# A finished right operand for the output product, made behind FFN 1 and kept in DRAM

## The chip, the cores and the metric

The kernel runs on one core of a Trainium2 chip. Compared is the device time of one execution in microseconds, the median of several runs of the whole layer, inputs and output in DRAM.

## The reference

One layer over 1024 tokens of width 1024, float32. The change touches the product with `w_out`; what it moves lies behind the first feed-forward block.

```python
h = h + 0.5 * swiglu(rms_norm(h, n1), w_gate1, w_up1, w_down1)           # FFN 1
z = rms_norm(h, nm) @ w_in                                              # q, k, v and two gates
merged = sigmoid(gA) * (yA @ w_branch_a) + sigmoid(gB) * (yB @ w_branch_b)
h = h + merged @ w_out                                                  # the output product
h = h + 0.5 * swiglu(rms_norm(h, n2), w_gate2, w_up2, w_down2)           # FFN 2
y = rms_norm(h, nf)
```

## The kernel before

**Precision.** Every operand of a large product is kept as two halves, hi (a cast to float32r) and lo (the rest), and a product of 128 x 128 by 128 x 512 is three matmuls into one PSUM bank: L149 hi by hi, L151 and L153 hi by lo and lo by hi. `split` makes the halves of a 128 x 512 operand: ACT casts hi (L95), DVE subtracts lo (L98). In FFN 1 the same is done by L325 and L332.

**Products.** Large products are Strassen-like: seven products P1 to P7 of quarter matrices in place of eight. Class `Down` does one for each W_down and one, the *merge*, for `w_out`. The merge's inner size is 4 blocks, so it has 28 entries (7 products by 4), taken in the order P2, P1, P5, P6, P3, P7, P4. For an entry `prep` makes a pair of tiles, the left operand `s` (a quarter of `merged`, or a sum that was put into `left_d`) and the right operand `t` (a block of `w_out`, or a difference of blocks), each 128 x 1024 with hi and lo side by side. Pairs stand in a ring of six: four of `ws` tiles, two inside the large tile `ar` (`pair_slots`). `run` prepares entry e + 5 before it multiplies entry e, and each entry is four times three matmuls. The last four entries are multiplied in `tail`, later.

**The right operand before.** `load_blocks` fetches the four quarters of `w_out` during branch A in eight transfers of 512 KB (L567) into two `ar` tiles. `prep` forms the differences in place on DVE: one subtraction per entry of P5 (L590) and P3 (L595), two per entry of P6 (L592, L593), so 16 in all; then it splits the left and the right operand (L95, L98).

**FFN 1.** It has 154 products, and after each `behind_ffn1(n)` is called with the number n that are left. It slips work in that belongs to later stages. 28 *items* (16 branch weights, 12 halves of gate weights) are each fetched (256 KB, L756 on SP), split two products later (ACT L760, DVE L761, both into small tiles `hs`, six in all), and put one product later by two transfers of 256 KB (L768, Pool's queue) to `wab_d` or `wg_d`. One item is begun every third product. From n = 10 on, `down.at_end` loads and prepares the product with W_down of FFN 1, one part of which stands in the two tiles `xs`.

**Order.** Instructions run in program order on each engine. `pin` and the calls above set that order; each engine waits for what its next instruction needs and nothing overtakes. DMAs are started by SP (loads and some stores) and Pool (puts), in order on each. The weights of FFN 1 are loaded by SP (L295), and its products are evicted by ACT (L477 and others) and DVE (L497 and others) out of PSUM banks; of the banks, the one in which P6 ends is written again soonest: P7's first matmul goes into it one product after P6's last.

Of the kernel before, what the change touches and what calls it, by code (L numbers as in the profile page):

```python
# [13 lines left out]
ALU = mybir.AluOpType  # L14
# [17 lines left out]
def f32v(ap):  # L32
    return ap.bitcast(F32)


@with_exitstack
def trunk_kernel(ctx, tc, x, xt, n1, wg1, wu1, wd1, nm, win, rpb, sink, wa, wb, wo,
                 n2, wg2, wu2, wd2, nf, c_rope, c_mask_a, c_mask_b, out):
    nc = tc.nc

# [13 lines left out]
    def nm_(s):  # L54
        uid[0] += 1
        return f"{s}_{uid[0]}"
# [32 lines left out]
    def ws4():  # L89
        return main.tile([P, 1024], F32R, tag="ws", bufs=8, name=nm_("ws"))  # L90
# [431 lines left out]
    def pair_slots(s):  # L522
        return slot(s), slot(s + 1)
# [8 lines left out]
    class Down:  # L532
# [2 lines left out]

        ORDER = ("P2", "P1", "P5", "P6", "P3", "P7", "P4")

        def __init__(self, n, w, scale, place, left=None, dram=None, loads={}, ring=(22, 24, 26), shift=0, late=False):
            self.n, self.w, self.scale, self.place, self.left, self.dram, self.loads = n, w, scale, place, left, dram, loads
            self.seq = [(k, p) for k in self.ORDER for p in range(n)]  # L540
            self.dk = [k for k in self.ORDER if k in dram]
            self.nd = (n + 1) // 2
            self.raw, self.nraw, self.done, self.ent, self.tiles, self.loaded = {}, 0, 0, {}, {}, {}
            self.TAIL, self.late = min(n, 5), late
            self.ring, self.shift, self.RING = ring, shift, 4 + len(ring)
            self.W = self.Y = None
# [32 lines left out]
        def prep(self, e):  # L579
            k, p = self.seq[e]  # L580
            if k in self.dram:
                d = self.dk.index(k) * self.nd + p // 2
                self.load_left(d + 3)
                left = self.raw[d][:, p % 2, :]
            else:
                left = self.left(k, p)
            b11, b12, b21, b22 = [self.blocks(n, p)[:, 0, :] if n in self.loaded else None for n in ("B11", "B12", "B21", "B22")]
            eng = nc.gpsimd if self.n > self.RING else nc.vector
            if k == "P5":
                nc.vector.tensor_tensor(b11, b12, b11, op=ALU.subtract)  # L590
            elif k == "P6":
                nc.vector.tensor_tensor(b11, b22, b11, op=ALU.subtract)  # L592
                eng.tensor_tensor(b12, b22, b12, op=ALU.subtract)  # L593
            elif k == "P3":
                eng.tensor_tensor(b21, b21, b11, op=ALU.subtract)  # L595
            i = (e + self.shift) % self.RING
            s, t = (ws4(), ws4()) if i < 4 else pair_slots(self.ring[i - 4])
            split(s[:, :512], s[:, 512:], left, None, self.late)
            split(t[:, :512], t[:, 512:], dict(B11=b11, B12=b12, B21=b21, B22=b22)[SOURCE[k]], None, self.late)
            self.ent[e] = s, t  # L600
# [145 lines left out]
    def hs(dt):  # L746
        return main.tile([P, 512], dt, tag="hs", bufs=6, name=nm_("hs"))
# [16 lines left out]
    def wab_put(i):  # L764
        g, half = divmod(i - 2 * NC8, 2)
        for k, a in enumerate(cast.pop(i)):
            dst = wab_d[i, :, k * 512:k * 512 + 512] if g < 0 else wg_d[g, k, :, half * 512:half * 512 + 512]
            nc.gpsimd.dma_start(dst, f32v(a))  # L768

    def behind_ffn1(n):  # L770
        down.at_end(n)
        if n <= 60 and spread:
            nc.sync.dma_start(*spread.pop(0))
        for e, f in ((3, wab_put), (2, wab_split), (0, wab_fetch)):
            i, k = divmod(100 - e - n, 3)
            if k == 0 and 0 <= i < 2 * (NC8 + len(gates)):
                f(i)

    hg = hidden(wg1, wu1, behind_ffn1, (8, 10, 9, 11), by_hand=True)

# [736 lines left out]
    def quarter(k, p):  # L1517
        m = merged(p + (4 if k in ("P2", "P4") else 0))
        return m[:, :512] if k in ("P1", "P2") else m[:, 512:]

    place = dict(B11=[(4, p) for p in range(4)], B21=[(4, 4 + p) for p in range(4)],
                 B12=[(1, p) for p in range(4)], B22=[(1, 4 + p) for p in range(4)])
    loads = {t: [lambda d, t=t: load_h(t)] for t in range(NTT)}
    loads[0].append(lambda d: d.load_left(2))
    down = Down(4, wo[0], 0.5, place, quarter, {k: left_d[i] for i, k in enumerate(("P5", "P6", "P3", "P7"))},
                loads, (8, 10), late=True)

    def combine(p):
        a11, a12, a22 = [quarter(k, p) for k in ("P1", "P2", "P4")]
# [7 lines left out]
    for i, dc in enumerate(a_order):  # L1537
        r = mix.pop(("ra", i))
        if i + 2 < NC8:
            a_fetch(i + 2)  # L1540
        if i >= 2:
            branch_a(i)
        if i % 2 == 0:
            down.load_blocks(("B21", "B11", "B12", "B22")[i // 2])
        if i + 3 == NC8:
            new_ar(2)
        if i + 1 == NC8:
            down.prep_until(2)
        bs, mm = a_mm[i]
        drain(mm)  # L1550
        if i + 6 < NC8:
            fetch_w(NC8 + i + 6)
        if i + 2 < NC8:
            a_open(i + 2)
        for n in range(2):
            sl = slice(n * 512, (n + 1) * 512)
            nc.vector.scalar_tensor_tensor(out=r[:, sl], in0=r[:, sl], scalar=1.0, in1=bs[n], op0=ALU.add, op1=ALU.mult)
        nc.vector.tensor_tensor(merged(dc), merged(dc), r, op=ALU.add)
        if i % 2:
            combine(i // 2)  # L1560
# [139 lines left out]
```

## Time and profile before

| | us |
|---|---|
| median of 3 runs | 1919.72 |
| lowest and highest run | 1918.26, 1920.03 |
| span of the profiled execution | 1915.6 |
| PE busy in it | 1905.7 (99%) |
| DVE, ACT, POOL busy | 1451.9 (76%), 947.5 (49%), 306.5 (16%) |
| DMA moved | 338.57 MB, 177 GB/s |

The profiled execution is given by its span, from its first instruction to its last; that span is 4.1 us shorter than the median of the runs, and what lies around it (launch and end) is in the runs' time and not in the profile. PE is TensorE's matmuls, whose ends are modelled, so a busy PE may still be spaced wider than it could be; the spacing of their starts tells. The waits of an engine are listed with what released them.

On the trace's clock FFN 1 runs from about 11 to 430 us, the branch products end at 1195.94, and the 24 entries of the merge before its tail run from there to about 1261.

### The profile page before, as it was taken

The page shows a single profiled execution, that of the slowest core. Times are in us where ns is not written, and L with a number is a line of the kernel's source. Part 1 is how long each engine was busy: PE and PEld are TensorE (multiplying, and loading weights), DVE is VectorE, ACT ScalarE, POOL GpSimd, SP SyncE. Part 2 cuts the span into 40 slices and gives each one's busy share as a digit, 9 for nine tenths or more (in the row PEclk, how much of TensorE's full clock was granted, in tenths as well). Part 3 has the DMA queues.
Part 4 walks back from the last instruction along what each step waited for, and adds up shares of the span by engine and source line. Part 5 has one row for each costly group of instructions (what it writes and reads, how often), then busy time and mean ns, then how long its engine had stood idle before and what let it go on. Part 6 is the DMA issues. An engine that isn't in the chain of part 4 may idle for free.

```text
span 1915.6 us, 25959 instructions
## 1 busy us (share of the span) xinstructions
PE 1905.7 (99%) x9044; PEld 1597.7 (83%) x9044; DVE 1451.9 (76%) x2545; ACT 947.5 (49%) x1847; POOL 306.5 (16%) x477
## 2 busy tenths in 40 slices
PE   9999999999999999999999999999999999999998
PEld 7888888888888888898898888888888888888886
DVE  8988766668967778755887997999675566569864
ACT  7533444444446543444888983475333333344453
POOL 0012222214400112211112201010110001005111
PEclk9999999999999999999999999999999999999999
DMA  7256656677354277753648978444432323492341
GB/s 269 95 175 217 231 200 219 205 277 284 115 180 141 105 213 236 226 176 127 176 117 228 283 225 309 171 154 133 142 110 97 118 88 110 157 357 86 119 140 61
DMA packets 174211, 338.57 MB, mean 177 GB/s; under 512 B 17280, under 2 KB 79616, under 8 KB 174080
## 3 DMA queue, kind: packets, MB, share of 16 engines
q1 hardware_dynamic: 140752, 235.18, 37.5%
q0 software_dynamic: 32464, 100.69, 15.6%
q8 instruction: 71, 1.16, 0.3%
q10 hardware_dynamic: 864, 1.05, 0.2%
q14 instruction: 60, 0.49, 0.1%
HBM read 230.43 MB, written 108.19 MB: 177 GB/s over the span
## 4 chain that ended last, share of the span: by engine, by line
PE 97%; DVE 1%; DMA 1%; ACT 0%; issue 0%; POOL 0%; SPq 0%; POOLq 0%; DVEq 0%; ACTq 0%
PE g L149 18%; PE g L153 17%; PE g L151 17%; PE d L153 12%; PE d L151 12%; PE d L149 12%; PE d L1438 2%; PE g L1457 1%; PE d L1417 1%; PE g L1452 1%; PE d L1418 1%; PE d L142 1%; DVE ar L98 0%; DMA fx<-in_xt_dram 0%; DMA fx<-v_d 0%
## 5 line engine op out<-in xcount | busy, mean ns | idle before, releaser
L149 PE MATMUL g<-ar,ws 128*128 128x512 f32 x1064 | 404.6, 393 | 0.0
L151 PE MATMUL g<-ar,ws 128*128 128x512 f32 x1064 | 401.8, 390 | 0.0
L153 PE MATMUL g<-ar,ws 128*128 128x512 f32 x1064 | 400.4, 390 | 0.0
L149 PE MATMUL d<-ar,ws 128*128 128x512 f32 x728 | 281.6, 390 | 0.4 <-ACT ar L908 0.4
L151 PE MATMUL d<-ar,ws 128*128 128x512 f32 x728 | 281.1, 389 | 0.6 <-DVE ar L910 0.6
L153 PE MATMUL d<-ar,ws 128*128 128x512 f32 x728 | 281.2, 389 | 0.0
L153 PEld LDWEIGHTS g<-ar,ws 128*128 128x128 f32 x1064 | 199.6, 188 | 41.6
L151 PEld LDWEIGHTS g<-ar,ws 128*128 128x128 f32 x1064 | 199.6, 188 | 41.0
L149 PEld LDWEIGHTS g<-ar,ws 128*128 128x128 f32 x1064 | 196.6, 188 | 35.9 <-DVE fa L1030 0.3
L332 DVE TENSOR_TENSOR ws<-raw,ws 128x512 fp32r<-128x512 f32 x216 | 147.6, 688 | 92.9 <-ACT ws L325 92.0
L325 ACT CAST ws<-raw 128x512 fp32r<-128x512 f32 x216 | 132.6, 620 | 149.6 <-PE g L153 67.0
L151 PEld LDWEIGHTS d<-ar,ws 128*128 128x128 f32 x728 | 136.7, 188 | 29.8 <-DVE ar L910 1.2
L149 PEld LDWEIGHTS d<-ar,ws 128*128 128x128 f32 x728 | 136.5, 188 | 28.9 <-ACT ar L908 0.9
L153 PEld LDWEIGHTS d<-ar,ws 128*128 128x128 f32 x728 | 136.6, 188 | 28.7 <-DVE ws L332 0.5
L95 ACT CAST ws<-raw 128x512 fp32r<-128x512 f32 x98 | 61.0, 623 | 119.2 <-PE d L153 59.9
L98 DVE TENSOR_TENSOR ws<-raw,ws 128x512 fp32r<-128x512 f32 x98 | 73.2, 747 | 44.3 <-ACT ws L95 44.2
L444 POOL DMA_DIRECT2D hid<-fx x91 | 49.2, 540 | 349.6 <-DVE fx L504 221.6
L98 DVE TENSOR_TENSOR ws<-ar,ws 128x512 fp32r<-128x512 f32 x114 | 93.5, 828 | 14.6 <-ACT ws L95 14.6
L95 ACT CAST ar<-raw 128x512 fp32r<-128x512 f32 (+1 forms) x81 | 54.0, 670 | 83.5 <-PE g L151 51.5
L149 PE MATMUL g<-ws,ws 128*128 128x512 f32 x232 | 90.9, 392 | 0.0
L153 PE MATMUL g<-ws,ws 128*128 128x512 f32 x232 | 90.4, 390 | 0.0
L151 PE MATMUL g<-ws,ws 128*128 128x512 f32 x232 | 90.3, 389 | 0.0
(344 smaller groups left out, 3830.9 us busy)
## 6 DMA issues: line engine op xcount, KB each, us to landing
raw<-hid SPq DMA_DIRECT2D x70, 512.0 KB
hid<-fx POOLq DMA_DIRECT2D x91, 256.0 KB, 2.7
ar<-in_ffn_w_down_dram SPq DMA_DIRECT2D x32, 512.0 KB
raw<-in_ffn_w_up_dram SPq DMA_DIRECT2D x31, 512.0 KB
raw<-in_ffn_w_gate_dram SPq DMA_DIRECT2D x27, 512.0 KB
hid<-fa POOLq DMA_DIRECT2D x51, 256.0 KB, 2.7
ar<-zs_d POOLq DMA_DIRECT2D x48, 256.0 KB, 7.5
raw<-in_w_in_dram SPq DMA_DIRECT2D x20, 512.0 KB
```

Source lines behind the costliest of these rows:

```text
L95: hi = nc.scalar.copy(dst_hi, src)
L98: (eng or nc.vector).tensor_tensor(dst_lo, src, f32v(dst_hi), op=ALU.subtract)
L142: nc.tensor.transpose(pt[:, c * P:(c + 1) * P], xs[:, (half * 4 + c) * P:(half * 4 + c + 1) * P], ident)
L149: nc.tensor.matmul(b, lhs[0], r[0], start=first, stop=False, **kw)
L151: nc.tensor.matmul(b, lhs[0], r[1], start=False, stop=False, **kw)
L153: nc.tensor.matmul(b, lhs[1], r[0], start=False, stop=last, **kw)
L325: nc.scalar.copy(w[0][:, :512], a)
L332: nc.vector.tensor_tensor(w[0][:, 512:], a, f32v(w[0][:, :512]), op=ALU.subtract)
L444: nc.gpsimd.dma_start(hid[PRODUCTS.index(p), i], src)
L1417: nc.tensor.matmul(b[:, :nw], un["q"][s], un["kd"][s][:, k0 * P:k1 * P], start=True, stop=False)
L1418: nc.tensor.matmul(b[:, :nw], un["q"][s], un["kl"][s][:, k0 * P:k1 * P], start=False, stop=True)
L1438: nc.tensor.transpose(pt[:, i * P:(i + 1) * P], un["pr"][s][:, i * P:(i + 1) * P], ident)
```

## The change

Three things are changed.

1. The items behind FFN 1 are begun every second product and no longer every third: item i is fetched at n = 108 - 2i (before: 100 - 3i). They end near n = 51, before: n = 16.
2. Behind them, from n of about 52 on, the right operand of the output product is made. For each of the four blocks p, four fetches of 256 KB bring the quarters of `w_out` into `hs` tiles (`wo_fetch`); then one entry is made every 1.5 products: a subtraction on DVE where the entry is a difference (16 in all, `wo_split`), a cast on ACT and a subtraction on DVE into one of three tiles that are idle there (`split_out`: two `xs` and the tile `gain`), and one product later one transfer of 512 KB, hi and lo side by side, on Pool's queue to `wo_d` (`wo_put`). The last put is called at n = 8.
3. In the merge, `prep` loads the finished `t` of an entry from `wo_d` with one transfer of 512 KB on SP and splits only the left operand. The eight loads of `w_out` in branch A are gone.

```diff
-            b11, b12, b21, b22 = [...]          # prep, before: always
+            if self.right is not None:
+                i = (e + self.shift) % self.RING
+                s, t = (ws4(), ws4()) if i < 4 else pair_slots(self.ring[i - 4])
+                nc.sync.dma_start(f32v(t), self.right[PRODUCTS.index(k), p])
+                split(s[:, :512], s[:, 512:], left, None, self.late)
+                self.ent[e] = s, t
+                return
...
+    wo_d = dram.tile([len(PRODUCTS), 4, P, 1024], F32, name="wo_d")
+    def halves_out():
+        nout[0] += 1
+        if nout[0] % 3 == 0:
+            return const.tile([P, 1152], F32R, tag="gain", bufs=1, name=nm_("made"))[:, :1024]
+        return main.tile([P, 1024], F32R, tag="xs", bufs=2, name=nm_("made"))
+    def split_out(key, src):
+        n = src.shape[1]
+        o = cast[key] = halves_out()[:, :2 * n]
+        pin(nc.scalar.copy(o[:, :n], src))
+        pin(nc.vector.tensor_tensor(o[:, n:], src, f32v(o[:, :n]), op=ALU.subtract))
+    def put_out(key, dst):
+        nc.gpsimd.dma_start(dst, f32v(cast.pop(key)))
+    def wo_fetch(p):
+        for n, (r0, c0) in dict(B21=(4, 0), B11=(0, 0), B22=(4, 512), B12=(0, 512)).items():
+            wo[n, p] = hs(F32)
+            nc.sync.dma_start(wo[n, p], wout[0][(r0 + p) * P:(r0 + p + 1) * P, c0:c0 + 512])
+    def wo_split(k, p):
+        for d, a, b in dict(P5=(("B11", "B12", "B11"),), P7=(("B12", "B22", "B12"),), P6=(("B11", "B22", "B11"),),
+                            P4=(("B21", "B21", "B11"),)).get(k, ()):
+            pin(nc.vector.tensor_tensor(wo[d, p], wo[a, p], wo[b, p], op=ALU.subtract))
+        split_out((k, p), wo[SOURCE[k], p])
...
+    for i in range(2 * (NC8 + len(gates))):
+        for e, f in ((3, wab_put), (2, wab_split), (0, wab_fetch)):
+            later(108 - 2 * i - e, f, i)
+    step = [50 - 1.5 * k for k in range(29)]
+    for p in range(4):
+        later(step[7 * p] + 2, wo_fetch, p)
+        for j, k in enumerate(("P2", "P1", "P3", "P5", "P7", "P6", "P4")):
+            later(step[7 * p + j], wo_split, k, p)
+            later(step[7 * p + j] - 1, wo_put, k, p)
...
-        for e, f in ((3, wab_put), (2, wab_split), (0, wab_fetch)):
-            i, k = divmod(100 - e - n, 3)
-            if k == 0 and 0 <= i < 2 * (NC8 + len(gates)):
-                f(i)
+        for f, *a in background.get(n, ()):
+            f(*a)
...
-    down = Down(4, wo[0], 0.5, place, quarter, {...}, loads, (8, 10), late=True)
+    down = Down(4, None, 0.5, {}, quarter, {...}, loads, (8, 10), late=True, right=wo_d)
...
-        if i % 2 == 0:
-            down.load_blocks(("B21", "B11", "B12", "B22")[i // 2])
```

How this moves the instructions is seen at three places. The order on PE is the same before and after, matmul for matmul.

ACT, in the last third of FFN 1, around copies of PSUM banks `d` and `g` into `fx` (L477); L325 is the cast of FFN 1's own weights. Before:

```order
L477 COPY fx_75<-d_2410 128x512
L325 CAST ws_2425<-fa 128x512
L477 COPY fx_76<-d_2428 128x512
L760 CAST hs_2443<-hs_2404 128x512
L325 CAST ws_2447<-raw_2177 128x512
L477 COPY fx_76<-g_2321 128x512
L325 CAST ws_2472<-raw_2468 128x512
L477 COPY fx_77<-g_2343 128x512
```

After:

```order
L477 COPY fx_75<-d_2511 128x512
L325 CAST ws_2528<-fa 128x512
L477 COPY fx_76<-d_2531 128x512
L793 CAST made_2546<-hs_2499 128x512
L325 CAST ws_2549<-raw_2260 128x512
L477 COPY fx_76<-g_2412 128x512
L325 CAST ws_2571<-raw_2567 128x512
L477 COPY fx_77<-g_2432 128x512
L793 CAST made_2588<-hs_2501 128x512
```

At this place a cast of the output product's first entry stands where an item's cast stood; the items are done by then, and from here a cast of L793 comes every 1.5 products, at times two of them in a row, where before one of L760 came every third.

SP, at the start of the merge: L576 (after: L577) loads sums from `left_d`, L1512 (L1568) loads rows of h, L295 loads weights of FFN 2. Before:

```order
L576 DMA raw_11129<-left_d 128x2x512
L1512 DMA fa<-h_d 128x1024 x2
L576 DMA raw_11131<-left_d 128x2x512
L576 DMA raw_11133<-left_d 128x2x512
L576 DMA raw_11206<-left_d 128x2x512
L1512 DMA fa<-h_d 128x1024 x2
L576 DMA raw_11256<-left_d 128x2x512
```

After:

```order
L577 DMA raw_11278<-left_d 128x2x512
L591 DMA ws_11285<-wo_d 128x1024
L591 DMA ws_11290<-wo_d 128x1024
L1568 DMA fa<-h_d 128x1024 x2
L591 DMA ws_11314<-wo_d 128x1024
L591 DMA ws_11332<-wo_d 128x1024
L577 DMA raw_11280<-left_d 128x2x512
L577 DMA raw_11282<-left_d 128x2x512
L577 DMA raw_11349<-left_d 128x2x512
L591 DMA ws_11352<-wo_d 128x1024
L591 DMA ws_11378<-wo_d 128x1024
```

The loads of finished operands (L591) stand between the loads of sums and of h, two to a load of sums, in the one queue.

DVE, in the merge, from the splits of P5's entries to the eviction of P1 out of bank `g` into `fx`. Before:

```order
L98 TENSOR_TENSOR ar_11005<-ar_10855,ar_11005 128x512
L590 TENSOR_TENSOR ar_10855<-ar_10970,ar_10855 128x512
L98 TENSOR_TENSOR ar_11005<-raw_11131,ar_11005 128x512
L592 TENSOR_TENSOR ar_10855<-ar_10970,ar_10855 128x512
L98 TENSOR_TENSOR ar_11005<-ar_10855,ar_11005 128x512
L593 TENSOR_TENSOR ar_10970<-ar_10970 128x512
L98 TENSOR_TENSOR ws_11298<-raw_11133,ws_11298 128x512
L98 TENSOR_TENSOR ws_11299<-ar_10855,ws_11299 128x512
L631 SCALAR_TENSOR_TENSOR fx_10848<-g_11231,fx_10848 128x512
```

After:

```order
L639 SCALAR_TENSOR_TENSOR fx_11012<-d_11276,fx_11012 128x512
L98 TENSOR_TENSOR ws_11351<-raw_11278,ws_11351 128x512
L98 TENSOR_TENSOR ws_11377<-raw_11278,ws_11377 128x512
L98 TENSOR_TENSOR ar_11158<-raw_11280,ar_11158 128x512 x2
L639 SCALAR_TENSOR_TENSOR fx_11009<-g_11372,fx_11009 128x512
```

The differences (L590, L592, L593) and the second split of each entry are gone from between the evictions; one split per entry stays.

## Rows read from the trace of the kernel before

**Rows 1.** The page: span, then busy time of each engine over the whole span.

```profile
span 1915.6 us, 25959 instructions
PE 1905.7 (99%) x9044; PEld 1597.7 (83%) x9044; DVE 1451.9 (76%) x2545; ACT 947.5 (49%) x1847; POOL 306.5 (16%) x477
```

**Rows 2.** All waits of PE: line, awaited, releaser: us in total, times, longest.

```profile
PE g L829 <- POOL ident masks.py:199: 1.5, 1, 1.5
PE d L151 <- DVE ar L910: 0.6, 2, 0.3
PE d L149 <- ACT ar L908: 0.4, 1, 0.4
PE d L1438 <- DVE ws L98: 0.2, 1, 0.2
```

**Rows 3.** Windows: us, then PE, PEld, DVE, ACT, POOL busy, clock, DMA share, GB/s.

```profile
133.00:293.00 160.00, 160.00 (x708) 132.48 (x707) 122.78 (x193) 63.88 (x110) 35.06 (x65) 1.00 0.62 210
293.00:408.00 115.00, 115.00 (x509) 95.24 (x508) 76.73 (x119) 47.92 (x84) 24.28 (x45) 1.00 0.63 212
...
1195.00:1260.00 65.00, 65.00 (x291) 53.67 (x290) 64.11 (x103) 30.51 (x56) 5.84 (x10) 1.00 0.52 182
...
1195.00:1217.00 22.00, 22.00 (x97) 17.94 (x96) 21.85 (x35) 9.24 (x17) 3.24 (x6) 1.00 0.73 256
```

**Rows 4.** Timeline of PE in the merge: start, duration, engine, line, operation, tiles.

```profile
1195.94 0.39 PE L149 MATMUL d<-ws,ws 128*128 128x512 f32 x1
...
1198.66 0.39 PE L149 MATMUL d<-ws,ws 128*128 128x512 f32 x1
...
1204.10 0.39 PE L149 MATMUL d<-ws,ws 128*128 128x512 f32 x1
1204.40 0.50 PE L151 MATMUL d<-ws,ws 128*128 128x512 f32 x1
...
1207.03 0.39 PE L149 MATMUL g<-ar 128*128 128x512 f32 x1
```

**Rows 5.** Timeline of DVE in the merge, same columns.

```profile
1203.67 0.68 DVE L98 TENSOR_TENSOR ws<-ar,ws 128x512 fp32r<-128x512 f32 x1
```

**Rows 6.** Groups by line, DVE and ACT, 293 to 408 us: busy, mean ns | idle before.

```profile
L761 DVE TENSOR_TENSOR hs<-hs,hs 128x512 fp32r<-128x512 f32 x12 | 8.3, 688 | 9.2 <-ACT hs L760 9.2
L760 ACT CAST hs<-hs 128x512 fp32r<-128x512 f32 x12 | 7.4, 617 | 0.0
```

**Rows 7.** Waits of ACT and of SP's queue in FFN 1, 133 to 408 us.

```profile
ACT ws L325 <- PE d L153: 46.7, 30, 2.1
...
SPq L756 <- DVE hs L761: 65.9, 13, 8.6
```

**Rows 8.** Timeline of ACT in FFN 1; in brackets the idle time before.

```profile
296.98 0.59 ACT L477 COPY fx<-g 128x512 f32<-128x512 f32 x1 [1.10 <-PE g L153]
```

**Rows 9.** DMA issues, 130 to 420 us: transfer, queue, count, KB each, us to landing.

```profile
wab_d<-hs POOLq DMA_DIRECT2D x32, 256.0 KB, 3.9
```

**Rows 10.** Groups by line, DVE and ACT, around the merge.

```profile
L98 DVE TENSOR_TENSOR ws<-ar,ws 128x512 fp32r<-128x512 f32 x25 | 16.5, 683 | 0.0
L590 DVE TENSOR_TENSOR ar<-ar,ar 128x512 f32<-128x512 f32 x4 | 2.7, 682 | 0.0
L95 ACT CAST ws<-ar 128x512 fp32r<-128x512 f32 x24 | 14.1, 618 | 22.6 <-PE d L153 9.5 <-DVE ar L592 6.7 <-DVE ar L590 5.8
```

**Rows 11.** DMA of 1150 to 1260 us in 40 slices (tenths, GB/s); a put.

```profile
DMA  9999988699899920468559945500614146055890
GB/s 326 399 411 386 366 317 311 191 339 388 353 410 419 411 94 0 164 206 268 229 159 384 421 180 197 188 2 0 197 36 154 19 171 191 4 186 180 346 408 25
DMA packets 9065, 25.95 MB, mean 236 GB/s; under 512 B 922, under 2 KB 922, under 8 KB 9056
...
left_d<-fa POOLq DMA_DIRECT2D x16, 256.0 KB, 5.6
```

**Rows 12.** Timeline of SP's queue at the merge.

```profile
1215.20 16.00 SPq L576 DMA_DIRECT2D raw<-left_d  x4
```

More of the change, by code (lines that the diff above doesn't have):

```diff
@@ L36, in trunk_kernel @@
 @with_exitstack
-def trunk_kernel(ctx, tc, x, xt, n1, wg1, wu1, wd1, nm, win, rpb, sink, wa, wb, wo,
+def trunk_kernel(ctx, tc, x, xt, n1, wg1, wu1, wd1, nm, win, rpb, sink, wa, wb, wout,
                  n2, wg2, wu2, wd2, nf, c_rope, c_mask_a, c_mask_b, out):
@@ L536, in trunk_kernel, with __init__ @@
         ORDER = ("P2", "P1", "P5", "P6", "P3", "P7", "P4")
-        def __init__(self, n, w, scale, place, left=None, dram=None, loads={}, ring=(22, 24, 26), shift=0, late=False):
+        def __init__(self, n, w, scale, place, left=None, dram=None, loads={}, ring=(22, 24, 26), shift=0, late=False, right=None):
+            self.right = right
             self.n, self.w, self.scale, self.place, self.left, self.dram, self.loads = n, w, scale, place, left, dram, loads
@@ L768, in wab_put, with wo_put, later @@
             nc.gpsimd.dma_start(dst, f32v(a))
+    wo_d = dram.tile([len(PRODUCTS), 4, P, 1024], F32, name="wo_d")
+    nout = [0]
+    wo = {}
+    def halves_out():
[19 more added lines that the diff above has]
+        split_out((k, p), wo[SOURCE[k], p])
+    def wo_put(k, p):
+        put_out((k, p), wo_d[PRODUCTS.index(k), p])
+    background = {}
+    def later(n, *f):
+        background.setdefault(int(n), []).append(f)
+    for i in range(2 * (NC8 + len(gates))):
[7 more added lines that the diff above has]
+            later(step[7 * p + j] - 1, wo_put, k, p)
     def behind_ffn1(n):
@@ L1519, in quarter @@
         return m[:, :512] if k in ("P1", "P2") else m[:, 512:]
-    place = dict(B11=[(4, p) for p in range(4)], B21=[(4, 4 + p) for p in range(4)],
-                 B12=[(1, p) for p in range(4)], B22=[(1, 4 + p) for p in range(4)])
     loads = {t: [lambda d, t=t: load_h(t)] for t in range(NTT)}
     loads[0].append(lambda d: d.load_left(2))
-    down = Down(4, wo[0], 0.5, place, quarter, {k: left_d[i] for i, k in enumerate(("P5", "P6", "P3", "P7"))},
-                loads, (8, 10), late=True)
+    down = Down(4, None, 0.5, {}, quarter, {k: left_d[i] for i, k in enumerate(("P5", "P6", "P3", "P7"))},
+                loads, (8, 10), late=True, right=wo_d)
     def combine(p):
```

## The prediction, made before the changed kernel ran

> **What bounds the kernel now.** I read the page first, then PE's waits, then windows over the three stretches that the change touches. PE is busy for 1905.7 of 1915.6 us [rows 1], and since ends of matmuls are modelled I looked at what it waits for: four rows in the whole span, 1.5 + 0.6 + 0.4 + 0.2 = 2.7 us, none of them at a line of FFN 1's steady part or of the merge [rows 2]. In the windows of FFN 1 (133 to 293 and 293 to 408 us) and of the merge (1195 to 1260) PE fills the stretch at clock 1.00, while DVE is at 77%, 67% and 99%, DMA at 0.62, 0.63 and 0.52 [rows 3]. The merge looks bound by DVE (64.11 of 65 us), and that is what the change relieves, so I looked at starts on PE there. From 1195.94 to 1198.66 are 12 matmuls, one entry: 2.72 us, 0.227 each. The entry that begins at 1204.10 takes until 1207.03, 2.93 us [rows 4]: its second matmul starts 0.30 us behind the first, its third later too. DVE made that entry's lo half from 1203.67 to 1204.35 [rows 5]. So DVE, busy as it is, has cost PE 0.21 us in the merge, once. Everywhere else it is in time. The kernel is bound by PE's own 9044 matmuls and loads of weights, and their order and number do not change: the sum is of what makes PE wait less or more.
>
> **FFN 1, added.** A split costs ACT 0.617 and DVE 0.688 us; that is the same operation on the same shape in an item of before, so I take that price for the new splits and for the new subtractions of 128 x 512 [rows 6]. New from about 293 us on: 28 casts, 28 x 0.617 = 17.3 us of ACT; 28 + 16 instructions of DVE, 44 x 0.688 = 30.3 us. Gone from there: 12 items, 7.4 us of ACT and 8.3 of DVE, which come earlier. In the last 115 us DVE then has 76.7 + 30.3 - 8.3 = 98.7 (86%) and ACT 47.9 + 17.3 - 7.4 = 57.8 (50%). In the 160 us before it, 12 items more give DVE 122.8 + 8.3 = 131.1 (82%) and ACT 63.9 + 7.4 = 71.3 (45%) [rows 3]. All of that lies beside PE. Its cover is that FFN 1's own casts run as far ahead as their slots go: ACT waited 30 times, 46.7 us, for PE to free one [rows 7]. If it were gone, the new work would cost what it lacks, but DVE and ACT keep 14% and 50% free, so on average nothing: 0.
>
> **FFN 1, transfers.** An item moves 0.26 MB in and 0.52 out. Twelve more before 293 us are 9.4 MB: 210 GB/s become (33.6 + 9.4) / 160 = 269. Behind it 16 fetches (4.2 MB) and 28 puts (14.7) take the place of 9.4: (24.4 - 9.4 + 18.9) / 115 = 295 GB/s, in place of 212 [rows 3]. Transfers reached 386 to 419 GB/s in other slices [rows 11], so these fit. A `made` tile is used again after three entries, 4.5 products or 12.2 us at 2.72 us each; its put is called one product behind its split, so it has 9.5 us to land, against 3.9 in the median for a put of half its size [rows 9]. Twice 3.9 would still be in time. Pool starts 28 puts instead of 24 in this stretch and was busy for 24.3 of 115 us.
>
> Here waits are added. SP starts four fetches in a row into six `hs` tiles, so some of them wait for the last splits of the block before, and FFN 1's loads of weights stand behind them. Of before, such waits of SP were 13 with 65.9 us in all and up to 8.6 each [rows 7], and PE waited for none [rows 2]. And ACT's L793 can wait for its tile or for a fetch, with copies out of PSUM behind it. The tightest is P6's: a copy of `g` starts at 296.98, ACT having waited 1.10 us for PE [rows 8], and P7 needs the bank one product (2.72 us) after P6's last matmul; less the copy's 0.59 that leaves some 2.1 us for what stands ahead of it. A cast or two that find their data (0.62 each) fit, a wait of 3 us doesn't. No row shows the new wait; from below it is 0, since L760 with the same lead of two products never waited (idle before it 0.0 [rows 6]); from above I take four entries that wait 1 us each past the slack, 4 us. I take 0.1, nearer to the row. A gain is excluded, as nothing is removed here that PE waited for.
>
> The loads of `gain` and of two `xs` blocks move behind the last puts. Both tiles are read only after more than 40 products of W_down or in the mixer (40 x 2.72 = 109 us), against 6 us for a transfer [rows 11]: 0.
>
> **Branch A.** Eight loads of 512 KB of `w_out` go (4.2 MB), six of finished operands come (3.1): SP and DMA get lighter. 0 on PE, whose waits are not here.
>
> **The merge.** Gone are 16 subtractions and 28 lo halves, 44 x 0.682 = 30.0 us of DVE (four lines of x4 like L590) and 28 x 0.618 = 17.3 of ACT [rows 10]: DVE falls from 64.1 to about 34 of 65 us. The worth of that on PE is the one delay, 0.21 us; between 0 and 0.2, I take 0.2. There is nothing else to win, as entries already start 2.72 us apart.
>
> Added: a load of 512 KB per entry. It can start when entry e - 6 has left its slot and must be there when e begins, five entries later, 13.6 us. A put of half the size took 5.6 us in the median in the loaded stretch [rows 11], so I leave 8 us for waiting behind others. From 1195 to 1217 seven loads come to 256 x 22 = 5.6 MB: 5.6 + 3.7 = 9.3 MB, 422 GB/s; from 1195 to 1260 22 loads come to 182 x 65 = 11.8 MB: 11.8 + 11.5 = 23.4 MB, 359 GB/s [rows 3]. The best slices with DMA at 9 tenths move 386 to 419, the poorest 326 [rows 11]. At 410, 0.7 us of backlog after the first 22 us, and none later; at 326, 28.5 less 22 = 6.5 us there and 71.8 - 65 = 6.8 us at the end. Both stay under 8. The price on PE is thus 0, with 0 as the lower bound and the second rival as the upper.
>
> The Trainium skill, "DMA: Bandwidth & Descriptors", section "Where 436 GB/s comes from", says that between HBM and SBUF the HBM side binds, at about 358 GB/s per core. Slices of 399 to 419 in this trace speak against it as a ceiling [rows 11]. By it the first 22 us would be short by 9.3 - 7.9 = 1.4 MB, an estimate of 4 us of backlog, which is under the 8 us too, but closer than by the row.
>
> SP's order matters as well. The loads stand two by two between loads of sums from `left_d`; of these, four are spread over 16 us, from 1215.20 on, each behind a tile that DVE must free [rows 12]. Entry 10's operand stands behind the first of them, 1215.2, and is used six entries behind entry 4's start of 1207.03 [rows 4], at 1207.03 + 6 x 2.72 = 1223.3: 8 us to land, and with DVE less busy the tile is free earlier. 0.
>
> **Sum.** 1915.6 in the profile's span: + 0.1 (FFN 1) + 0 (branch A) - 0.2 (merge) = 1915.5. The span lies 4.1 us under the median of the runs, so 1919.72 - 0.1 = **1919.6 us**. A measurement tells about 0.2% (3.8 us) from no change; this is the same time.
>
> **Rivals.**
> *The merge was bound by DVE after all.* For it: 64.11 of 65 us busy. Against it: starts at 0.227 us, one delay of 0.21. If every wait that PE has in rows 2 but the first (1.2 us) went as well, 1919.7 - 0.2 - 1.2 = 1918.3, which still is no measurable gain. To be faster by 3.8 us, matmuls would have to start closer than 0.227 us at an unchanged clock. 2 in 100.
> *The merge's transfers come late (slower).* It decides where finished operands come more than 8 us behind their turn: 23.4 MB must take over 73 us, a rate under 320 GB/s. For it: over the whole of 1150 to 1260 only 236 GB/s were moved (the mean of the slices), the new loads stand in one queue behind loads that wait, and 422 GB/s are wanted at first. Against it: that mean has idle slices in it, and no slice at 9 tenths was under 326. At 280 GB/s 83.6 - 65 - 8 = 10.6 us late: 1930. At 236, 99 - 73 = 26 us: 1946. 7 in 100, more near 1925 to 1930.
> *FFN 1's evictions are held (slower).* ACT's casts and DVE's pinned subtractions wait for fetches, or a put lands late, ahead of P6's copies. For it: DVE at 86%, DMA 40% up, four fetches in a row through six tiles. Against it: L760 never waited. Four entries at 1 us give 1923.6 and are within 0.2%; 8 of them, two a block, at 1 us, 1927.6. 5 in 100 for over 3.8 us.
> *The change doesn't do what it says:* the loads could all be held behind one wait of SP. They stand spread in its queue, two to a load of sums, so this has no chance of its own beside the second rival.
>
> **How the numbers follow.** My forecast, no change, has 86 in 100: 2 for the first rival, 7 and 5 for the slower ones. Within 0.2% is 0.86, faster 0.02, slower 0.12. The range: below, 1918.3 by the first rival, and the medians of three runs lie up to 1.5 us apart (1918.26 to 1920.03), so 1917.0; above, 1923.6 from FFN 1's upper bound, and 1926 takes in the smaller of the late transfers. What is left out is about 1 in 10 by the cases and I leave it so, the costs in FFN 1 being bounded by one row only.
>
> **What would show it.** PE's matmuls of one entry in the merge again 2.72 us apart, with no 2.93; DVE at about 34 of 65 us there, 99 of 115 in FFN 1's last stretch; DMA at about 360 GB/s in the merge and 295 in FFN 1; no wait of PE for `wo_d` loads or `ws` with a DMA as releaser, none for `fx` copies in FFN 1. Wrong would be: any such wait of over 1 us in all, entries of the merge over 2.8 us apart, or a change of the span that comes from a place in which nothing was changed.

## The result, and the profile after

The changed kernel takes 1922.32 us (median of 9 runs, 1920.85 to 1924.52), the kernel before in the same sessions 1918.26 (9 runs, 1917.36 to 1920.03): 1.0021 of it, interval 1.0012 to 1.0031. It is slower by about 4 us, or 0.2%. I had forecast no change, 1919.6.

The page of the changed kernel, span and engines, beside [rows 1]:

```profile
span 1920.5 us, 26141 instructions
PE 1907.5 (99%) x9044; PEld 1598.8 (83%) x9044; DVE 1454.0 (76%) x2545; ACT 947.2 (49%) x1847; POOL 323.0 (17%) x505
```

The span grew by 4.9 us, PE's busy time by 1.8 only; the same 9044 matmuls now wait. All waits of PE in the changed kernel (line, awaited, releaser: us in total, times, longest), beside [rows 2]:

```profile
PE g L149 <- ACT fx L477: 2.0, 1, 2.0
PE g L885 <- POOL ident masks.py:199: 1.5, 1, 1.5
PE d L151 <- DVE ws L98: 1.0, 1, 1.0
PE d L151 <- DVE ar L98: 0.9, 1, 0.9
PE d L151 <- DVE ar L966: 0.3, 1, 0.3
PE d L1494 <- DVE ws L98: 0.2, 1, 0.2
```

Three are new: one for a copy on ACT (2.0), two for lo halves on DVE (1.0 and 0.9). The windows say where (us, then busy us of PE, PEld, DVE, ACT, POOL, clock, DMA share, GB/s), beside [rows 3]:

```profile
133.00:293.00 160.00, 157.99 (x698) 130.53 (x697) 127.37 (x203) 68.52 (x120) 46.88 (x87) 1.00 0.75 255
293.00:408.00 115.00, 115.00 (x509) 95.27 (x508) 94.44 (x151) 56.41 (x99) 26.74 (x50) 1.00 0.74 272
408.00:460.00 52.00, 52.00 (x231) 43.09 (x230) 32.05 (x52) 23.53 (x43) 3.96 (x8) 1.00 0.98 368
460.00:525.00 65.00, 63.03 (x276) 51.30 (x275) 64.66 (x69) 26.12 (x47) 43.16 (x22) 1.00 0.51 173
...
1200.00:1265.00 65.00, 65.00 (x293) 53.93 (x292) 38.01 (x56) 17.79 (x31) 4.84 (x8) 1.00 0.93 336
```

PE loses 2 us between 133 and 293, where items now come every second product, and 2 us between 460 and 525, in the product with W_down, which I hadn't looked at. It loses nothing in 293 to 408, where most of the new work lies, and nothing in the merge, where DVE fell from 64.1 to 38.0 of 65 us and transfers rose from 182 to 336 GB/s.

To compare kernels I use one more figure, worked out from the timeline: the **loss** of a stretch is the sum of what matmul starts stand wider apart than 0.227 us, over the pairs wider than 0.240. Before, it is 0.1 us in 20 to 440, 0 in 440 to 540 and 0.5 in the merge (1190 to 1270). After, it is 2.4, 2.8 and 0.2. The sum of the differences is 2.3 + 2.8 - 0.3 = 4.8 us, which is the span's 4.9.

**The first loss, 223 us.** The end of product P6, on PE (start, duration, engine, line, tiles, idle before and its releaser):

```profile
223.14 0.39 PE L153 MATMUL g<-ar,ws 128*128 128x512 f32 x1
225.54 0.50 PE L149 MATMUL g<-ar,ws 128*128 128x512 f32 x1 [2.01 <-ACT fx L477]
```

On ACT at that time:

```profile
218.61 0.62 ACT L325 CAST ws<-fa 128x512 fp32r<-128x512 f32 x1
224.38 0.62 ACT L768 CAST hs<-hs 128x512 fp32r<-128x512 f32 x1 [5.15 <-DMA hs<-in_w_branch_a_dram]
224.91 0.58 ACT L477 COPY fx<-g 128x512 f32<-128x512 f32 x1
```

And on SP's queue, from which that fetch comes:

```profile
209.64 0.37 SPq L764 DMA_DIRECT2D hs<-in_w_branch_a_dram  x1
...
215.66 0.34 SPq L295 DMA_DIRECT2D raw<-in_ffn_w_up_dram  x1
217.46 0.34 SPq L295 DMA_DIRECT2D fa<-in_ffn_w_gate_dram  x1
217.89 0.39 SPq L764 DMA_DIRECT2D hs<-in_w_branch_a_dram  x1
```

ACT had nothing to do for 5.15 us: the cast of an item, put into its order two products behind the fetch, waits for that fetch, and the copy that frees P7's bank stands behind the cast. The fetch went out at 217.89 only, since SP stood until 215.66 at a load of FFN 1's weights (a wait of 5.6 us for DVE) and until 217.46 at the next, and landed some 6.4 us later.

**The second loss, 516 to 525 us.** In the product with W_down, Pool forms differences of right operands (L593; after: L601) beside the subtractions of DVE. Its first ones, before and after (start, duration, engine, line, tiles, idle before and its releaser):

```profile
457.00 7.84 POOL L593 TENSOR_TENSOR ar<-ar,ar 128x512 f32<-128x512 f32 x5 [23.58 <-DMA raw<-hid]
```

```profile
467.44 16.63 POOL L601 TENSOR_TENSOR ar<-ar,ar 128x512 f32<-128x512 f32 x7 [28.41 <-DMA ar<-in_ffn_w_down_dram]
```

Pool begins 10.4 us later; with the 2.3 us taken off that PE itself is late by then, 8.1. It waits, by the trace, for one of W_down's loads. SP started the last of these into `ar` at 453.78 us and just after in the kernel before, at 463.99 and just after in the changed one:

```profile
453.78 1.44 SPq L567 DMA_DIRECT2D ar<-in_ffn_w_down_dram  x3
```

```profile
463.99 1.02 SPq L568 DMA_DIRECT2D ar<-in_ffn_w_down_dram  x2
```

DMA is still full then, where it was half idle before (460 to 470 us, before and after):

```profile
460.00:470.00 10.00, 10.00 (x46) 8.28 (x45) 10.00 (x16) 4.57 (x8) 6.50 (x5) 1.00 0.49 163
```

```profile
460.00:470.00 10.00, 10.00 (x45) 8.27 (x45) 9.96 (x18) 4.36 (x8) 2.56 (x1) 1.00 1.05 387
```

It matters when Pool begins, since a subtraction on DVE takes 1.66 to 1.79 us and not 0.68 when it meets one on Pool (last section). DVE has no idle time from 460 us on in either kernel (64.7 of 65 us), and the same 41 instructions stand from its first group of evictions in this product to the second. The two groups, before, then after:

```profile
460.75 2.47 DVE L631 SCALAR_TENSOR_TENSOR fx<-d,fx 128x512 f32<-128x512 f32 x4
498.56 2.47 DVE L631 SCALAR_TENSOR_TENSOR fx<-g,fx 128x512 f32<-128x512 f32 x4
```

```profile
462.09 2.48 DVE L639 SCALAR_TENSOR_TENSOR fx<-d,fx 128x512 f32<-128x512 f32 x4
504.17 2.47 DVE L639 SCALAR_TENSOR_TENSOR fx<-g,fx 128x512 f32<-128x512 f32 x4
```

The 41 instructions take 37.8 us before and 42.1 after; of the single subtractions of 128 x 512 among them, 11 are long ones before and 14 after. So DVE enters this stretch 1.3 us later than before, which is less than the 2.3 us of PE, and leaves it 5.6 us later: the lateness is made inside it. PE meets it behind 516 us; DVE, then PE:

```profile
516.31 1.77 DVE L98 TENSOR_TENSOR ws<-ar,ws 128x512 fp32r<-128x512 f32 x1
```

```profile
516.72 0.39 PE L149 MATMUL d<-ws,ws 128*128 128x512 f32 x1
518.13 0.50 PE L151 MATMUL d<-ws,ws 128*128 128x512 f32 x1 [1.03 <-DVE ws L98]
```

ACT's waits between 400 and 460 us are longer as well (6.5 us for `raw<-hid` and 4.2 for a load of W_down; before, 1.8 and 1.4), but they are not the way to this loss, since DVE is not late against PE when it comes to 460 us.

The same two windows of the kernel before show how little room there was: DMA at 0.97 of its time from 408 to 460, and DVE full behind it.

```profile
408.00:460.00 52.00, 52.00 (x232) 43.03 (x231) 34.02 (x53) 23.15 (x41) 6.24 (x8) 1.00 0.97 360
460.00:525.00 65.00, 65.00 (x288) 53.85 (x287) 64.69 (x76) 27.44 (x48) 38.52 (x21) 1.00 0.38 122
```

### The profile page after: what moved, and what is told of

Its sections match the earlier page's. It is cut to its first block, busy times and chain, and to the rows that moved or that the text cites. A ratio compares the mean times of both kernels' runs of the same rounds, so it can differ in the third digit from the quotient of the medians.

```text
span 1920.5 us, 26141 instructions
## 1 busy us (share of the span) xinstructions
PE 1907.5 (99%) x9044; PEld 1598.8 (83%) x9044; DVE 1454.0 (76%) x2545; ACT 947.2 (49%) x1847; POOL 323.0 (17%) x505
## 4 chain that ended last, share of the span: by engine, by line
PE 95%; DVE 2%; DMA 1%; issue 0%; ACT 0%; SPq 0%; POOLq 0%; POOL 0%; DVEq 0%; ACTq 0%
PE g L149 18%; PE g L151 18%; PE g L153 17%; PE d L151 12%; PE d L153 12%; PE d L149 12%; PE d L1494 2%; PE g L1513 1%; PE d L1473 1%; PE g L1508 1%; PE d L1474 1%; DMA hs<-in_w_branch_a_dram 1%; PE d L142 1%; DVE ar L98 0%; DVE ws L98 0%
## 5 line engine op out<-in xcount | busy, mean ns | idle before, releaser
L325 ACT CAST ws<-raw 128x512 fp32r<-128x512 f32 x216 | 132.5, 620 | 135.8 <-PE g L153 62.8
L98 DVE TENSOR_TENSOR ws<-ar,ws 128x512 fp32r<-128x512 f32 x94 | 80.7, 859 | 16.7 <-ACT ws L95 16.7
```

What stands on the lines that cost most here:

```text
L98: (eng or nc.vector).tensor_tensor(dst_lo, src, f32v(dst_hi), op=ALU.subtract)
L325: nc.scalar.copy(w[0][:, :512], a)
```

## The experiments

All are compared with the kernel before, run beside them. The losses of all runs (us, as defined above) stand in one table; two profiles of one kernel differ by up to 1.1 us in 440 to 540 (lead3) and 1.7 in the merge (held_only). The last two columns belong to the second loss: by how much Pool's first subtraction there starts later than before, less what PE is late by then, and the time of DVE's 41 instructions.

| kernel | ratio, interval | 20 to 440 | 440 to 540 | 1190 to 1270 | Pool later | DVE's 41 |
|---|---|---|---|---|---|---|
| before | | 0.1 | 0 | 0.5 | 0 | 37.8 |
| changed | 1.0021, 1.0012 to 1.0031 | 2.4 | 2.8 | 0.2 | 8.1 | 42.1 |
| items2 | 1.0014, 1.0005 to 1.0024 | 1.8 | 0 | 0.8 | 0.3 | 38.1 |
| lead3 (twice) | 1.0014, 1.0005 to 1.0023 | 0.1, 0.1 | 3.6, 2.5 | 0.3, 0.3 | 8.3, 6.9 | 42.1, 42.1 |
| early6 | 1.0002, 0.9992 to 1.0012 | 0.6 | 0.7 | 0.4 | 1.8 | 40.3 |
| early6_lead3 | 1.0006, 0.9997 to 1.0015 | 0.1 | 1.3 | 0.4 | 3.0 | 40.9 |
| held_only (twice) | 1.0012, 1.0002 to 1.0022 | 0.1, 0.1 | 1.7, 1.4 | 0.8, 2.5 | 3.3, 3.2 | 41.3, 41.1 |
| puts_only | 1.0011, 1.0001 to 1.0021 | 0.1 | 2.4 | 0.5 | 4.3 | 42.1 |
| no_puts | 1.0006, 0.9996 to 1.0017 | 0.1 | 0.7 | 1.3 | 1.5 | 39.2 |
| dve_late | 1.0007, 0.9997 to 1.0016 | 0.1 | 1.5 | 0.8 | 1.1 | 35.4 (47) |
| merge_double | 1.0033, 1.0021 to 1.0045 | 0.5 | 0.7 | 3.0 | 1.9 | 40.3 |
| early12 | 1.0048, 1.0031 to 1.0065 | 8.7 | 0 | 0.1 | 0.4 | 38.1 |
| tight | 1.0003, 0.9994 to 1.0013 | 0.2 | 0 | 0.4 | -0.4 | 36.7 |

Over all profiles but dve_late's, whose DVE has other work, the second loss goes with Pool's start: 0 where it is up to 0.4 us later, 0.7 at 1.5 to 1.9, 1.3 to 1.7 at 3.0 to 3.3, 2.4 at 4.3, and 2.5 to 3.6 at 6.9 to 8.3. No run delays Pool alone, so this route is read from the traces and not shown by an edit of its own.

**Only the items closer together (items2).** An edit of the kernel before:

```diff
-            i, k = divmod(100 - e - n, 3)
+            i, k = divmod(108 - e - n, 2)
```

> The kernel before, with only the items behind FFN 1 begun every second product (from n = 108) and not every third; nothing of w_out is made there and the merge is as before. Theory: the changed kernel's wait of PE at 223 us (a copy of P6 on ACT stands behind a cast that waits 5.15 us for an item's fetch) comes from this density alone, so it is here again: one wait of about 2 us, the span some 2.2 us over the kernel before (1.0011 of it), no wait at 516 to 525 us, and in the merge the entry of 2.93 us is back. Rival, that the work of w_out behind the items is the cause of both: no wait of PE over 0.3 us in FFN 1, the same time as before.

Its waits of PE between 20 and 600 us are one:

```profile
PE g L149 <- ACT fx L477: 1.0, 1, 1.0
```

It is the copy at 223 us, with ACT waiting 4.1 us for the fetch of an item of `w_branch_a`. The density of the items makes the first loss, and the second is none of it. The size came out smaller than expected (1.8 us of loss, not 2.2; 0.4 of it lies at 262 us). ACT waits here for W_down's loads as well (2.6 and 1.7 us between 396 and 480 us), longer than before and without a loss behind it.

**A longer lead for the fetches (lead3).** An edit of the changed kernel:

```diff
-            later(108 - 2 * i - e, f, i)
+            later(108 - 2 * i - e + (e == 0), f, i)
```

> The changed kernel with each item's fetch called three products ahead of its split, not two. Theory: the wait at 223 us is a fetch that SP starts late behind FFN 1's weight loads and that lands 5 to 6 us later; one product (2.72 us) more lead takes most of it away, PE's waits in FFN 1 fall from 2.0 to under 0.5 us, the waits at 516 to 525 us stay (2.9 us in matmul starts), so the kernel is 2 us faster than the changed one and 2.5 to 3 us slower than before. Rival, that DVE and ACT have no room there whatever the fetches: a wait of 2 us stays, or moves to another of P6's copies.

The first loss is gone, 0.1 us. But the kernel was only 1.4 us faster than the changed one (1920.94 against 1922.32). The second loss came out at 3.6 us, and at 2.5 in the profile taken again, against 2.8; the intervals of the two ratios overlap, so it isn't shown that the second loss grew by what the first gave back.

> The kernel of the run lead3 once more, for the scatter of one profile to the next: 3.6 us lost between 440 and 540 us again, within 0.7 us, if a difference of 1 us between two kernels there is to mean anything.

The scatter of 1.1 us is larger than I allowed for; I draw nothing from differences under that in one profile.

**All of it earlier (early6, early6_lead3).**

```diff
-            later(108 - 2 * i - e, f, i)
+            later(114 - 2 * i - e, f, i)
...
-    step = [50 - 1.5 * k for k in range(29)]
+    step = [56 - 1.5 * k for k in range(29)]
```

> The changed kernel with all work behind FFN 1 six products (16 us) earlier: items from n = 114, entries of w_out from step 56, the last put at n = 14 and not 8. Theory: the waits at 516 to 525 us begin at 408 to 425 us, where the last four puts (2.1 MB, 5 us of DMA) lie with the loads of W_down and make ACT wait 4.2 us (before: 1.4) for one of them; ended 16 us earlier they leave the loads alone, so these waits (2.9 us) go. The wait of 2 us for an item's fetch may stay, move or go. Expected: 2 to 3 us faster than the changed kernel, with the first wait left; the same time as before within 0.1% if that goes too. Rival, that the two xs loads and the gain load behind the puts are the cause: they still are in the loaded stretch in part, and 1 us or more of the waits stays.

The second loss fell from 2.8 to 0.7 us, the first from 2.4 to 0.6 (at another place, 262 us), and the time is that of before. early6_lead3 has the `(e == 0)` of lead3 as well:

> Both: work behind FFN 1 six products earlier, and items fetched three products ahead of their split. Theory: with both causes gone no wait of PE over 0.3 us is left between 20 and 1200 us, and only the merge's gain of 0.2 us is there: the kernel's time before, between 0.9995 and 1.0003 of it. Rival, that the added work costs PE something that these two waits don't show (transfers against matmuls' reads): 1 us or more slower than before without a wait.

The time, 1.0006 of before, is above the 0.9995 to 1.0003 that I expected (its own interval begins at 0.9997), and a loss of 1.3 us stayed at the second place, against my "no wait over 0.3 us" (one of 0.7). With the last put at n = 14 the second cause isn't gone.

**Which part makes the second loss (held_only, puts_only, no_puts).** All three start from lead3 and do the merge as before. held_only makes nothing of `w_out`, it only holds the three tiles:

```diff
+    def fill():
+        for _ in range(3):
+            made.append(halves_out())
+            pin(nc.scalar.copy(made[-1][:, :4], nhalf4))
+    def empty():
+        for t in made:
+            pin(nc.scalar.copy(hs(F32R)[:, :4], t[:, :4]))
+    later(52, fill)
+    later(8, empty)
```

> The run lead3 (the changed kernel, items fetched three products ahead) without the fetches, splits and puts of w_out; the three tiles are taken at n = 52 and given back at n = 8 by copies of 4 columns, so that the loads of gain (0.5 MB) and of the last blocks of W_down (four of 256 KB) stand where the change puts them. The merge splits both operands as before. It asks whether these moved loads alone cost PE anything between 440 and 530 us, where lead3 loses some 4 us in matmul starts. Theory that the puts collide with W_down's loads: under 0.5 us there. Rival, that the loads moved into the fullest stretch do it: 2 us or more.

It lost 1.7 us and, once more, 1.4. That is no "under 0.5": holding the tiles alone, with no added transfer and no work, costs about half of what lead3 loses. What it does is to move loads: those of `gain` and of four blocks of W_down (1.5 MB) are started at 221 to 225 us in the kernel before, at 419 and 465 to 472 in the changed one, and at 415 and 460 to 470 here, in and behind the stretch that is full. DVE comes to its first evictions 1.4 us earlier than before (459.39), ACT's waits for W_down's loads are shorter (1.6 us in all, before 2.3), and still DVE's 41 instructions take 41.3 us. What is late is Pool's start, by 3.3 us, behind a load of W_down.

> The kernel of the run held_only once more, for the scatter: 1.7 us lost between 440 and 540 us again, within 0.7 us. If it comes out near 0.7, as without the puts, then the loads that were moved and the added work of DVE can't be told apart.

puts_only has 28 puts of 512 KB from tiles filled once (`touch` copies 4 columns into the tile):

```diff
+    def put_made(i):
+        nc.gpsimd.dma_start(wo_d[i // 4, i % 4], f32v(made[i % 3]))
...
+    later(52, fill)
+    for i in range(28):
+        later(step[i], touch, i)
+        later(step[i] - 1, put_made, i)
```

> As held_only, with the 28 puts of 512 KB at the places where the change has them, from three tiles filled once (a copy of 4 columns into each tile ahead of its put keeps the order); no fetches of w_out, no splits or subtractions. The merge as before. Theory, puts collide with W_down's loads from n = 10 on: 2 to 4 us of waits between 440 and 530 us, as in lead3. Rival, that DVE's and ACT's added work delays W_down's first splits: as in held_only.

It lost 2.4 us, held tiles and puts together; lead3 itself lost 2.5 to 3.6. How much the puts add to the held tiles (0.7 to 1.0 us by these profiles) is under the scatter and stays open. no_puts has the fetches, subtractions and splits, and no put:

```diff
-            later(step[7 * p + j] - 1, wo_put, k, p)
```

> lead3 with the fetches, subtractions and splits of w_out, but without the 28 puts; the merge as before. Theory, puts collide: under 1 us of waits between 440 and 530 us. Rival, the added work of DVE and ACT: 2 to 4 us there.

It lost 0.7 us. So DVE's and ACT's added work is not what makes the loss; the rival falls. That it lost less than held_only, though its tiles are also held (until about n = 9), isn't explained by a run, and the difference is under the scatter; in the traces its load of `gain` is started at 405.00 us, in held_only at 415.49, and Pool's first subtraction is less late (1.5 against 3.3 us).

**How lateness of DVE reaches PE (dve_late).** Into the kernel before, in `prep` of the product with W_down, for one entry:

```diff
+                for _ in range(6):
+                    nc.vector.tensor_tensor(t[:, 512:], dict(B11=b11, B12=b12, B21=b21, B22=b22)[SOURCE[k]], f32v(t[:, :512]),
+                                            op=ALU.subtract)
```

> The kernel before, with six more subtractions of 128 x 512 on DVE in the product with W_down of FFN 1, near 467 us (the lo half of one right operand is made seven times, with the same result): 6 x 0.60 = 3.6 us of DVE, no transfers, nothing else. Theory: from 459 to 525 us DVE of the kernel before has no idle time, and its lo halves are some 2.2 us ahead of PE at 512 us (made at 512.47, wanted by L151 at 514.66), so whatever makes DVE late at its start is handed on in full but for these 2.2 us: PE waits 1.4 us (1 to 2) near 514 to 521 us, the span is 1.4 us longer. Rival, that DVE has more room than that or that the waits need late transfers too: no wait over 0.3 us, the span as before.

Loss 1.5 us between 511 and 521 us, no other new wait of PE up to there; 1.4 had been worked out. The wait of that kernel:

```profile
PE d L151 <- DVE ws L98: 0.7, 2, 0.4
```

The number agrees by luck, as the lateness didn't travel as the theory has it. With six instructions more, DVE took 35.4 us from its first evictions to its second, less than the 37.8 before, and was there 1.9 us earlier than before (496.69 against 498.56). In that time two subtractions on Pool, which took 6.99 us before, took 20.57:

```profile
468.84 20.57 POOL L595 TENSOR_TENSOR ar<-ar,ar 128x512 f32<-128x512 f32 x2 [3.50 <-DVE ar L592]
```

DVE fell behind only after that, when Pool caught up: its next 36 instructions, to the third evictions at 528.07, took 31.4 us and 27.8 before. So the run shows that DVE and Pool hold each other up there, and that PE waits once DVE is late. It doesn't show that lateness from 467 us is handed on, nor how much room DVE has then.

**Twice as early (early12).** Items from n = 120 with lead3's fetches, `step = 62 - 1.5 k`.

> The changed kernel with all work behind FFN 1 twelve products (33 us) earlier, the last put at n = 20, items fetched three products ahead of their split. Theory: the later the puts and the tiles they hold end, the more of it meets W_down's loads from n = 10 on: the loss between 440 and 540 us was 3.6 us with the last put at n = 8, 1.3 at n = 14, and should be under 0.4 at n = 20; the span then that of before less the merge's gain, 1915.4 to 1916.0. Rival, that what is left at n = 14 doesn't depend on when the puts end (more work of DVE in the stretch, other order on SP): 1 us or more stays. Third, a wait in FFN 1 of 1 us or more, since items now begin in a stretch in which DVE is at 93%.

The second loss is 0, as the theory wanted: 3.6 or 2.5, 1.3, 0 with the last put at n = 8, 14, 20. The third case came true as well, with more than I had thought:

```profile
PE g L149 <- DVE fx L479: 6.0, 1, 6.0
```

This is another bank held, at 158 us, by an eviction on DVE. PE is 8.5 us late from there on, which could be what helps the second place; tight, the next run, shows the same 0 without that wait.

**Neither cause (tight).** early6_lead3 with an entry every 1.25 products:

```diff
-    step = [56 - 1.5 * k for k in range(29)]
+    step = [56 - 1.25 * k for k in range(29)]
```

> The run early6_lead3 (work behind FFN 1 six products earlier, items fetched three products ahead) with one entry of w_out every 1.25 products and not every 1.5, so that the last put is at n = 21, and items still begin at n = 114. Theory: with the fetches ahead nothing is lost between 20 and 440 us, and with the puts and held tiles gone before W_down's loads nothing between 440 and 540 (under 0.3 us each); the merge keeps its gain of 0.2 to 0.4 us. Span 1915.2 to 1916.2, time the same as before (0.9994 to 1.0004). Rival, that DVE, at 28 x 1.08 us of new work in 35 products and no more 42, now holds FFN 1's own splits or copies: 1 us or more lost between 290 and 400 us.

No wait of PE is left that the kernel before hadn't of its kind; all of them:

```profile
PE g L885 <- POOL ident masks.py:199: 1.5, 1, 1.5
PE d L151 <- DVE ar L966: 0.6, 2, 0.3
PE d L149 <- ACT ar L964: 0.4, 1, 0.4
PE d L1494 <- DVE ws L98: 0.2, 1, 0.2
```

The losses are 0.2 and 0, and the time that of before, 1.0003 (0.9994 to 1.0013). Pool begins its subtractions at 457.14 us, as in the kernel before (457.00). The two losses are all that the change costs, and without them it brings nothing that can be measured. The span of 1916.5 is above the 1915.2 to 1916.2 I had named. No version here beats the kernel before.

**How much cover the merge's transfers have (merge_double).** In early6, beside each load in `prep`:

```diff
+                for c in range(2):
+                    nc.sync.dma_start(hs(F32), self.right[PRODUCTS.index(k), p, :, c * 512:c * 512 + 512])
```

> The run early6 (all work behind FFN 1 six products earlier) with the merge's loads of finished operands doubled: beside each load of 512 KB two of 256 KB of the same data go into hs tiles that nothing reads. It asks how much cover the merge's transfers have. 22 loads more make 23.4 + 11.5 = 35 MB in 65 us, 537 GB/s, over the 386 to 419 GB/s of full slices. Theory, the prediction's own (8 us of lead): 35 / 0.41 = 85 us, 20 us of backlog, so PE waits some 10 us in the merge. Rival, that the loads have far more lead than that, or that the doubled ones are spread into the time after the merge: under 3 us.

The merge's window and three of the waits of PE:

```profile
1195.00:1260.00 65.00, 62.66 (x276) 51.30 (x275) 38.70 (x58) 16.43 (x28) 6.37 (x11) 1.00 1.00 382
```

```profile
PE g L149 <- ACT ws L325: 2.5, 1, 2.5
PE d L149 <- DMA ws<-wo_d: 1.6, 1, 1.6
PE g L149 <- DMA ws<-wo_d: 0.8, 1, 0.8
```

Now operands do come late, the rival mechanism exists. In the merge 3.0 us are lost; with a wait of 2.5 us for FFN 2's first weights behind it and one of 1.8 for `wab_d` ahead of it the span of this profile is 7.9 us over early6's; by the ratios (1.0033 against 1.0002) the difference is some 6 us. That is between the two cases I had named, 10 and under 3. The changed kernel has no such wait at a DMA share of 0.93 in its merge; where between single and doubled loads the cover ends was not tried.

## Why the prediction was wrong

**What bounds the kernel: right.** PE's matmuls and nothing else; the change could only lose, beyond a few tenths.

**The merge: right.** Entries start 2.72 us apart throughout; the fourth entry, which took 2.93 before [rows 4], in the changed kernel:

```profile
1209.42 0.39 PE L149 MATMUL d<-ws,ws 128*128 128x512 f32 x1
...
1212.14 0.39 PE L149 MATMUL g<-ar 128*128 128x512 f32 x1
```

DVE was at 38 of 65 us (34 forecast), transfers at 336 GB/s (359). The gain of 0.2 us was read from one profile; over the seven profiles with the merge as before the loss there was 0.5 to 2.5 us (mean 1.0), over the seven with finished operands and no doubled loads 0.1 to 0.4 (mean 0.3). It is nearer 0.8 than 0.2, and still under what a measurement shows; what is left with finished operands are matmuls behind transposes of the next stage, and no entry of the merge is delayed. The second rival, late transfers, did not occur: the lead of 8 us was enough.

**FFN 1 behind 293 us: right.** DVE at 94.4 of 115 us (98.7 forecast), ACT at 56.4 (57.8), 272 GB/s (295), no wait of PE. The four fetches through six tiles, the tightest place I named, cost nothing.

**FFN 1 ahead of 293 us: the step that failed first.** I priced twelve more items there as averages, DVE at 82% and ACT at 45%, and called it 0. The averages came out (80% and 43%), the price did not. The mechanism that I described, a cast on ACT ahead of P6's copies waiting for its data, with some 2.1 us of slack, is what happened (a wait of 5.15 us of ACT, 2.0 of PE), but I had placed it behind 293 us, with the new casts, and priced it at 0.1 by [rows 6], a row of 293 to 408. That row showed that items every third product found their data. It said nothing of items every second one, whose fetches stand closer behind SP's waits for slots.

**`gain` and the two `xs` tiles, "0": the step that failed second.** I compared 109 us of lead with 6 us for a transfer. The lead was misread: Pool takes the two `xs` tiles from 475.3 us on in the kernel before and from 484.0 in the changed one, 12 us behind the last of their loads. Even so no engine waited for these tiles. What cost was that their transfers and the last puts keep DMA full past 470 us, behind 408 us, a stretch I never opened, where DMA was already at 0.97: Pool begins its subtractions there 8.1 us later against PE, three more of DVE's subtractions fall beside them, and PE loses 2.8 us. The sum had no term for the product with W_down at all, so neither of the slower rivals nor the bound of 4 us for FFN 1 could stand for it. How the 2.8 us divide between moved loads and puts stays open.

**The numbers.** Of the lost 5.1 us (2.3 + 2.8), the upper bound for FFN 1 (4 us) held the first part. The time lies in the range, 1917.0 to 1926.0, but by luck: its upper end was made of four waits behind 293 us and of late transfers in the merge, neither of which came, and slower had only 12 in 100. The first and second rivals did not come true; the third did in its mechanism, at another place and with 2.3 us, and another cause stood beside it. The prediction's own sign of being wrong, a wait of over 1 us for `fx` copies in FFN 1, is there (2.0 us). The 4.1 us from span to median are too much as well: in the runs here each time is 1.7 to 2.4 us above its own span, so the rest was scatter between runs, and 1915.5 us of span would have given some 1917.5.

## What to carry to other kernels

Work that is moved behind another stage is priced in every stretch that it or what it displaces passes through, and not only where it is put: open the windows of the stretches next to it, look at which of them has DMA near 1.0 or an engine without idle time, and ask which loads were standing early in a tile that is now taken. A share of busy time says nothing of a queue in order: for each cast or copy on the path, ask how long ahead its transfer is *started*, what SP waits for just before that, and which eviction stands behind the cast. Where a background task is made denser, a row taken at the old density is no bound. And where two engines hold each other up, a load that is late for the one costs time on the other: look at when both are at work, and not only at the engine that PE waits for.

## What the runs showed of the hardware

A subtraction of 128 x 512 on DVE with both operands in SBUF took 0.68 us, and 1.78 beside a subtraction on Pool; of the kernel before, DVE and then Pool:

```profile
490.20 0.68 DVE L98 TENSOR_TENSOR ar<-raw,ar 128x512 fp32r<-128x512 f32 x1
490.81 1.78 DVE L98 TENSOR_TENSOR ar<-ar,ar 128x512 fp32r<-128x512 f32 x1
```

```profile
490.43 1.61 POOL L595 TENSOR_TENSOR ar<-ar,ar 128x512 f32<-128x512 f32 x1 [1.42 <-DVE ar L592]
```

Started 0.38 us into Pool's instruction, DVE's is 1.1 us longer. The Trainium skill, "SBUF — State Buffer", section "SBUF: two separate sides", says that DVE and GpSimd share a port pair as an exclusive lock, which an operation of DVE with two SBUF inputs contends for against a GpSimd operation that reads SBUF, and that the second waits for the first to end. The trace agrees to within 0.13 us: 490.43 + 1.61 = 492.04, and 492.04 + 0.68 = 492.72, where 490.81 + 1.78 = 492.59. From 460.75 to 526.39 us 17 single subtractions of DVE are long ones in the kernel before; at 0.68 us each they would take some 18 us less (an estimate), so DVE would have idle time there.

The doubled loads moved 382 GB/s over the 65 us of the merge, as a mean. This is above the figure of about 358 that the Trainium skill, "DMA: Bandwidth & Descriptors", section "Where 436 GB/s comes from", gives for the HBM side and that the prediction cited; as in [rows 11], the measurement decides.

In the first profile of lead3, behind a wait of PE of 1.76 us, the granted clock is 0.50 (1.2 of 2.4 GHz) for a while and eight matmuls start 0.39 to 0.43 us apart; they make some 1.6 of its 3.6 us. In the changed kernel it stays at 1.00 behind the wait of 2.01 us.

```profile
517.25:520.60 3.35, 3.35 (x9) 2.63 (x8) 3.32 (x4) 1.14 (x2) 1.84 (x2) 0.50 0.46 90
```
